# A sample's cache pages in a hybrid decoder step: all key scores ahead of most value pages, low parts through PSUM

## The chip, the cores and the metric

The kernel runs on 1 core of one Trainium2 chip. The metric is the device time of one execution in microseconds (us), the median of several. One profiled execution has its own time, and the tables say which of the two a number is.

## The reference

One step of a two-layer decoder: a Mamba-2 layer and an FFN, then one shared key/value projection, differential attention over it, and a second FFN. It computes this for a prompt of 16 + 512 tokens and for 8 sample tokens. Each sample token also attends to its past of 2048 tokens, which lies in a paged cache, 16 pages of 128 tokens for keys and as many for values, so 128 key pages and 128 value pages in all.

```python
def swiglu(x, w_gate, w_up, w_down):
    return (jax.nn.silu(x @ w_gate) * (x @ w_up)) @ w_down

def diff_attn_sample(h, k_past, v_past, k_new, v_new, pos, w_q, lam_vecs, subln_w, w_o, lambda_init):
    q = rotary((h @ w_q).reshape(b, T, DIFF_HEADS, 2, DIFF_QK_DIM), pos)
    s_past = jnp.einsum('bqhcd,bkhcd->bhcqk', q, k_past) * scale
    s_new = jnp.einsum('bqhcd,bkhcd->bhcqk', q, k_new) * scale
    w = diff_weights(jnp.concatenate([s_past, s_new], axis=-1), lam)   # softmax, map 0 - lam * map 1
    o = (jnp.einsum('bhqk,bkhe->bqhe', w[..., :P], v_past)
         + jnp.einsum('bhqk,bkhe->bqhe', w[..., P:], v_new))
    return diff_output(o, subln_w, w_o, lambda_init)
...
    # layer 0: mamba2, post_norm, swiglu, post_norm -> shared_kv
    # layer 1: attention, post_norm, swiglu, post_norm
```

## The kernel before

Activations are stored transposed: 128 partitions by T = 536 columns (528 prompt, 8 sample). A matrix product of full precision is made of three passes over rounded operands, high by high, low by high and high by low (`unit`, L121). For that each weight tile of up to 128x1024 comes as `raw` by a DMA of ACT's queue (L192), ACT copies it to `whi` with rounding (L200), and DVE, or POOL during the attention, subtracts: `wlo` = `raw` - `whi` (L202). Activations are split alike by `split`, high part on ACT (L242), low part on DVE (L243).

An FFN stage is one block of 128 hidden columns: the gate's product in PSUM, Silu on ACT into `sg` (L919), the up product in PSUM, `sg` times that product on DVE back into `sg` (L925), and the split of `sg`. The down products are added to the residual on DVE (L871, L872, in the last group L941) and shifted (L255); sums for the norm go on DVE or POOL (L268, L269). The norm `ln` subtracts and scales (L288, L290), applies weight and bias (L303) and makes high and low parts (L305), the latter as `x2lo` for the attention.

The sample tokens run ahead of the prompt: `early` takes their columns through the first FFN and the query projection while the prompt is still behind, and then starts `decode`. That is a generator with one step for each page. A step loads key page n+2 into one of 3 slots (a DMA of SP), multiplies key page n by the broadcast query on POOL (L1152), sums over 64 elements on DVE into the score tile `sc` (L1153), and takes value page n-24 (3 slots of its own) with four matmuls into PSUM bank `ps_e` (L125; the trace shows 8 records for a page). Every 16 key pages a softmax over them is spawned (L1174 to L1191), every 16 value pages the output of a sample is copied out (L1204).

The order on PE, DVE, ACT and POOL is made at build time: generators carry a modelled PE time, and whatever is behind it is pumped (here 3.2 for each step of `decode`) between the groups of the main flow, then a scheduler with priorities arranges each engine's row. SP's row is in program order. On the chip each engine takes its row in order and waits on semaphores.

`attention` takes heads 0 to 7: projections of k, v, q, rotation (L1348 to L1351), the split of `qk`, the score maps, the values. At its start the phase "attn" moves low parts of weights to POOL. Before the product with `w_o` it must have all of `decode` behind it: the operands `ohi` and `olo` lie in the same memory as the page slots (`r5`, `dd`). The end of the sample's attention (`fin`, L1513 to L1545) is joined within the `w_o` stage.

Of the kernel before, what the change touches and what calls it, by code (L numbers as in the profile page):

```python
# [10 lines left out]
F32 = mybir.dt.float32  # L11
# [4 lines left out]
ALU = mybir.AluOpType  # L16
AX = mybir.AxisListType.X
# [3 lines left out]
P = 128  # L21
# [12 lines left out]

NE = 24
MSP = 15

ES0 = 24

# [71 lines left out]
class Kernel:  # L111
# [68 lines left out]
    def wensure(self, load, split):  # L180
        nc = self.nc
        while self.wload < min(load, len(self.wq)):
            name, m, k0, k1 = self.wq[self.wload]
            n = k1 - k0
            mw = 32 if name == "w_dt" else P
            raw = self.wpool.tile([P, 8, P], F32, tag="raw", name="raw", bufs=3)
            if n == 2:
                n = 8
                src = self.i[name][m:m + 4][:, :, k0:k1, :].rearrange("m p k c -> p m (k c)")
                nc.scalar.dma_start(out=raw.rearrange("p (m k) c -> p m (k c)", k=2), in_=src)  # L190
            else:
                nc.scalar.dma_start(out=raw[:, :n, :mw], in_=self.i[name][m][:, k0:k1, :])  # L192
            self.wt[self.wload] = (raw, n, mw)
            self.wload += 1
        while self.wsplit < min(split, len(self.wq)):
            raw, n, mw = self.wt[self.wsplit]
            hi = self.wpool.tile([P, 8, P], F32R, tag="whi", name="whi", bufs=4)
            lo = self.wpool.tile([P, 8, P], F32R, tag="wlo", name="wlo", bufs=4)
            r = raw[:, :n, :mw]
            nc.scalar.copy(hi[:, :n, :mw], r)  # L200
            eng = self.lo_engine()
            eng.tensor_tensor(out=lo[:, :n, :mw], in0=r, in1=hi[:, :n, :mw].bitcast(F32), op=ALU.subtract)  # L202
            self.wt[self.wsplit] = (hi, lo, n, mw)
            self.wsplit += 1

# [128 lines left out]
    def build(self):  # L334
        nc, tc = self.nc, self.tc
        with ExitStack() as ctx:
            self.cp = ctx.enter_context(tc.tile_pool(name="const", bufs=1))
            self.wpool = ctx.enter_context(tc.tile_pool(name="wts", bufs=1))
            self.rp = ctx.enter_context(tc.tile_pool(name="regions", bufs=1))
            self.dp = ctx.enter_context(tc.tile_pool(name="scratch", bufs=1, space=DRAM))  # L340
            self.pp = ctx.enter_context(tc.tile_pool(name="psum", bufs=1, space=PSUM))
            self.gi, self.gn = 0, 3
            self.wi = 0
            self.lnps = "ab"
            self.lastexp = None
            self.phase = "mixer"
            self.wplan()
            self.consts()
            with tc.tile_pool(name="mixer", bufs=1, side="right") as mp:
                self.mp = mp  # L350
                self.mixer()
            with tc.tile_pool(name="rest", bufs=1, side="right") as sp:
                self.sp = sp
                self.rest()
# [432 lines left out]
    def rest(self):  # L787
# [52 lines left out]
            t2[0] = self.region("R6", [P, 8, T], F32, "t1")  # L840
            return t2[0]

        gens = self.ffn(x1k, FW, mk_t0, lnf0, gens, after_first=lnps, lasth=FH)
        S.finish(self.early_gen)

        self.attention(x2, gens)
# [27 lines left out]
    def proj(self, groups, xk, halves, evac, lnf, lasth=None):  # L874


        gens = []
        for gi, grp in enumerate(groups):
            last = gi == len(groups) - 1
            chs = [self.wget(nc_) for _, nc_ in grp]  # L880
            if not last:
                self.wahead(min(2, 4 - sum(n for _, n in grp)))
            for hf, (c0, n) in enumerate((lasth or halves) if last else halves):
                for (m, _), ch in zip(grp, chs):
                    ps = self.gps()
                    self.unit(ps, ch, xk, (c0, n))
                    evac(m, ps, c0, n)
                if last:
                    gens.append(self.S.spawn(lnf(hf, c0, n)) if lnf else None)
        self.wahead(2)  # L890
        return gens

    def ffn(self, xk, halves, mk_t, lnf, gens, after_first=None, lasth=None, regs=("R0", "R1")):
        nc, S, sp = self.nc, self.S, self.sp
        V, A = nc.vector, nc.scalar
        t = None
        for part in range(2):
# [5 lines left out]
            j = 0  # L903
            while j < 11:
# [5 lines left out]
                for hf, (c0, n) in enumerate((lasth or halves) if first else halves):  # L910
                    if first:
                        S.finish(gens[hf])
                        if hf == 1 and after_first is not None:
                            after_first()
                    for jj, (cg, cu) in zip(grp, chs):
                        pg, pu = self.gps(), None
                        self.unit(pg, [cg], xk, (c0, n))
                        sg = self.scr(n)
                        si = A.activation(sg, pg[:, :n], AF.Silu)  # L919
                        if self.lastexp is not None:  # L920
                            self.order(self.lastexp, si)
                            self.lastexp = None
                        pu = self.gps()
                        self.unit(pu, [cu], xk, (c0, n))
                        V.tensor_tensor(out=sg, in0=sg, in1=pu[:, :n], op=ALU.mult)  # L925
                        hh, hl = hk(jj)
                        self.split(hh[:, c0:c0 + n], hl[:, c0:c0 + n], sg)
                if first:
                    self.wahead(2)
                j += len(grp)  # L930
# [13 lines left out]
            if part == 0:  # L944
                self.proj([[(m, 2)] for m in range(8)], hk, halves, evac, None)
            else:
                gens = self.proj([[(m, 2)] for m in range(6)] + [[(6, 2), (7, 2)]], hk, halves, evac, lnf, lasth)
        return gens


# [48 lines left out]
    def early(self, t):  # L999
# [103 lines left out]
        for j in range(4):  # L1103
            nc.sync.dma_start(out=bass.AP(tensor=q.tensor, offset=q.offset + 256 * j, ap=[[1024, 8], [1, 256]]),
                              in_=qr[32 * j:32 * j + 8, :])
        yield 3.0
        self.dec_gen = S.spawn(self.decode(), 0.0)

    def page(self, cache, n, slot):
# [3 lines left out]


    def decode(self):
        nc, S, i, sp = self.nc, self.S, self.i, self.sp
        V, A, G = nc.vector, nc.scalar, nc.gpsimd
        kslot = self.kslot
        vslot = [self.r5[:, 1, :], self.r5[:, 2, :], self.r5[:, 3, :]]
        qslot = [self.dd[:, 2, :], self.dd[:, 3, :]]  # L1120
        self.Mb = sp.tile([P, 8, 16], F32, name="Mb", tag="Mb")
        self.Sb = sp.tile([P, 8, 16], F32, name="Sb", tag="Sb")
        self.oT = sp.tile([P, 8, 16], F32, name="oT", tag="oT")
        kq, vq = {}, {}
        N = 128

        def qload(b):
            q = self.scr_q
# [4 lines left out]
        VL = 24  # L1133
        w = {}
        sc = None
        qload(0)
        for n in range(N + VL + 1):
            if n < N:
                b, p = divmod(n, 16)
                if p == 8 and b < 7:  # L1140
                    qload(b + 1)
                if p == 0:
                    sc = sp.tile([P, 288], F32, tag="sc", name="sc", bufs=3)
                    V.memset(sc[:, 256:], 0.0)
                if n + 2 < N:
                    page("cache_k", n + 2, kslot[(n + 2) % 3])
            v = n - VL
            if 0 <= v + 2 < N:
                page("cache_v", v + 2, vslot[(v + 2) % 3])
            if n < N:  # L1150
                kt = kslot[n % 3]
                G.tensor_tensor(out=kt, in0=kt, in1=qslot[b % 2], op=ALU.mult)  # L1152
                V.reduce_sum(sc[:, 16 * p:16 * p + 16], kt.rearrange("p (c d) -> p c d", d=64), axis=AX)  # L1153
            if v >= 0 and v < N:
                bv, pv = divmod(v, 16)
                if pv == 0:
                    pe = self.ps("e")
                vt = vslot[v % 3]
                for j in range(4):
                    self.mmf(pe[32 * j:32 * j + 32, :256], w[bv][:, 16 * pv:16 * pv + 32],  # L1160
                             vt[:, 256 * j:256 * j + 256], start=pv == 0, stop=pv == 15, share=4)
                if pv == 15:
                    S.spawn(self.dec_out(bv, pe), 0.5)
            yield 3.2
            if n < N and p == 15:
                w[b] = sc
                S.spawn(self.dec_softmax(b, sc), 0.0)

    def dec_softmax(self, b, sc):
        nc, sp = self.nc, self.sp  # L1170
# [36 lines left out]
    def attention(self, x2, gens):  # L1207
# [1 line left out]
        V, A, G = nc.vector, nc.scalar, nc.gpsimd  # L1209
        self.gn = 2  # L1210
        self.gi = 0
        self.phase = "attn"
        self.xi = 0
        a4 = self.four("R4a", F32, "att4")
        b4 = self.four("R4b", F32, "att4b")
# [57 lines left out]
        for h in range(8):  # L1273
            if h == 0:
                chs = [self.wget(1) for _ in range(3)]
                for hf in range(2):
# [3 lines left out]
                    V.tensor_tensor(out=x2["l"][:, :, d], in0=x, in1=x2["h"][:, :, d].bitcast(F32), op=ALU.subtract)  # L1280
                    for wi in range(3):
                        kvq(h, wi, chs[wi], hf)
            else:
                for wi in range(3):
                    ch = self.wget(1)
# [371 lines left out]
```

## Time and profile before

| | us |
|---|---|
| median of 3 executions | 1830.72 (1823.65 to 1832.97) |
| profiled execution | 1819.79 |
| its span | 1818.0 |
| PE busy in it | 1667.7 (92%) |
| DVE busy | 1169.8 (64%) |
| ACT busy | 768.3 (42%) |
| POOL busy | 572.6 (31%) |
| mean granted TensorE clock | 0.958 |

The page multiplications begin at 614 us and end near 1157; the first FFN's matmuls end near 994; the norm runs to 1051; head 0 takes until about 1120, the other heads to 1320, `w_o` and its norm to 1440, and the second FFN from there to 1800. Busy shares of PE overlap: a matmul is recorded for longer than the next one waits for it.

### The profile page before, as it was taken

The numbers are of one execution on the slowest core, as the hardware profiler recorded it, in microseconds if no ns is written. First come the engines' busy times: TensorE is split into PE (matmuls) and PEld (weight loads), VectorE is DVE, ScalarE is ACT, GpSimd is POOL, SyncE is SP. The second block draws the span as 40 slices with busy tenths as digits, with TensorE's granted clock in tenths as the row PEclk, the third lists the DMA queues.
The fourth block names the chain that finished last, engine by engine and source line by source line (L and its number), as shares of the span: only waits on it lengthen the run. The fifth ranks groups of instructions, "written<-read, shape, count | busy, mean of one in ns | idle before, by whom it ended". The sixth has DMA issues, their size and how long they took to land.

```text
span 1818.0 us, 32096 instructions
## 1 busy us (share of the span) xinstructions
PE 1667.7 (92%) x12232; PEld 1404.1 (77%) x12232; DVE 1169.8 (64%) x1837; ACT 768.3 (42%) x1578; POOL 572.6 (31%) x402
## 2 busy tenths in 40 slices
PE   7799998989999989999998686999987999999996
PEld 7788887877776766666666473679976899999995
DVE  5498877854362589966677969757778533443334
ACT  6978868252352322222223322455644432223223
POOL 0010011100150487555678485412225400000025
PEclk9899999999999999999999696999999999999998
DMA  5675565397969679989898586761202222332221
GB/s 179 164 220 184 174 205 178 131 218 271 314 205 378 213 247 360 346 306 332 315 326 312 193 329 220 277 225 68 72 31 81 71 93 72 92 117 93 76 81 55
DMA packets 156801, 355.50 MB, mean 196 GB/s; under 512 B 23509, under 2 KB 74118, under 8 KB 156518
## 3 DMA queue, kind: packets, MB, share of 16 engines
q1 hardware_dynamic: 116902, 228.26, 37.7%
q10 hardware_dynamic: 36944, 116.59, 19.1%
q0 software_dynamic: 2800, 8.60, 1.4%
q8 instruction: 96, 1.57, 0.3%
q14 instruction: 59, 0.48, 0.1%
HBM read 337.07 MB, written 16.52 MB: 194 GB/s over the span
## 4 chain that ended last, share of the span: by engine, by line
PE 60%; DVE 17%; DMA 8%; ACT 7%; POOL 4%; issue 4%; SPq 1%; ACTq 0%; POOLq 0%; DVEq 0%
PE ps_g L121 48%; PE ps_e L125 3%; DVE sc L1153 2%; PE ps_a L125 2%; DVE wlo L202 2%; PE ps_d L125 2%; ACT acsb L677 1%; PE ps_c L125 1%; DMA out_conv_s<-cv 1%; DMA acsb<-scr_chk 1%; POOL dd L1152 1%; POOL ln_xf L303 1%; ACT whi L200 1%; PE ps_b L121 1%; DMA dd<-in_cache_k 1%
## 5 line engine op out<-in xcount | busy, mean ns | idle before, releaser
L200 ACT CAST whi<-raw 128x1024 fp32r<-128x1024 f32 (+3 forms) x243 | 234.6, 967 | 476.1 <-PE ps_g L121 404.4
L202 DVE TENSOR_TENSOR wlo<-raw,whi 128x1024 fp32r<-128x1024 f32 (+2 forms) x211 | 276.7, 1313 | 200.1 <-ACT whi L200 197.2
L1152 POOL TENSOR_TENSOR dd<-dd 128x1024 f32<-128x1024 f32 x85 | 215.8, 2543 | 102.7 <-DMA dd<-in_cache_k 88.4
L121 PE MATMUL ps_g<-xhi,whi 128*128 128x268 f32 (+1 forms) x656 | 194.9, 297 | 14.3 <-ACT xhi L242 9.4
L121 PE MATMUL ps_g<-x3hi,whi 128*128 128x260 f32 x704 | 200.1, 285 | 3.8 <-ACT sgw L919 3.3
L121 PE MATMUL ps_g<-x3lo,whi 128*128 128x260 f32 x704 | 199.5, 284 | 0.3 <-POOL x3lo L305 0.3
L121 PE MATMUL ps_g<-x3hi,wlo 128*128 128x260 f32 x704 | 199.1, 283 | 0.0
L121 PE MATMUL ps_g<-xhi,wlo 128*128 128x268 f32 (+1 forms) x656 | 196.5, 300 | 0.0
L121 PE MATMUL ps_g<-xlo,whi 128*128 128x268 f32 (+1 forms) x656 | 194.0, 296 | 0.1
L121 PE MATMUL ps_g<-x1hi,whi 128*128 128x512 f32 (+1 forms) x384 | 148.2, 386 | 4.1 <-ACT sgw L919 4.1
L121 PE MATMUL ps_g<-x1lo,whi 128*128 128x512 f32 (+1 forms) x384 | 148.6, 387 | 3.3 <-POOL x1lo L305 3.2
L121 PE MATMUL ps_g<-x1hi,wlo 128*128 128x512 f32 (+1 forms) x384 | 147.3, 384 | 0.0
L1152 POOL TENSOR_TENSOR r<-r,dd 128x1024 f32<-128x1024 f32 x43 | 107.8, 2508 | 113.9 <-DMA dd<-in_cache_k 75.7
L121 PEld LDWEIGHTS ps_g<-xhi,whi 128*128 128x128 f32 (+1 forms) x656 | 125.6, 192 | 22.7 <-ACT xhi L242 9.4
L121 PEld LDWEIGHTS ps_g<-x3hi,whi 128*128 128x128 f32 x704 | 132.8, 189 | 4.5 <-ACT sgw L919 3.7
L121 PEld LDWEIGHTS ps_g<-x3lo,whi 128*128 128x128 f32 x704 | 133.3, 189 | 0.5 <-POOL x3lo L305 0.5
L121 PEld LDWEIGHTS ps_g<-x3hi,wlo 128*128 128x128 f32 x704 | 133.5, 190 | 0.0
L121 PEld LDWEIGHTS ps_g<-xhi,wlo 128*128 128x128 f32 (+1 forms) x656 | 125.2, 191 | 7.5 <-issue 7.1
L121 PEld LDWEIGHTS ps_g<-xlo,whi 128*128 128x128 f32 (+1 forms) x656 | 125.6, 191 | 3.9 <-issue 2.8
L121 PE MATMUL ps_g<-hlo,whi 128*128 128x260 f32 (+2 forms) x400 | 126.7, 317 | 0.0
L121 PE MATMUL ps_g<-hhi,whi 128*128 128x260 f32 (+2 forms) x400 | 126.2, 316 | 0.0
L121 PE MATMUL ps_g<-hhi,wlo 128*128 128x260 f32 (+2 forms) x400 | 126.2, 316 | 0.0
(523 smaller groups left out, 4181.0 us busy)
## 6 DMA issues: line engine op xcount, KB each, us to landing
r<-in_cache_v SPq DMA_DIRECT2D x128, 512.0 KB, 5.1
dd<-in_cache_k SPq DMA_DIRECT2D x85, 512.0 KB, 5.3
raw<-in_w_gate ACTq DMA_DIRECT2D x44, 512.0 KB, 3.8
raw<-in_w_up ACTq DMA_DIRECT2D x44, 512.0 KB, 5.7
r<-in_cache_k SPq DMA_DIRECT2D x43, 512.0 KB, 5.3
raw<-in_w_in ACTq DMA_DIRECT2D x40, 512.0 KB, 3.8
raw<-in_w_down ACTq DMA_DIRECT2D x32, 384.0 KB, 3.3
raw<-in_w_down ACTq DMA_DIRECT2D x32, 320.0 KB, 5.4
```

The costliest lines, as they stand in the source:

```text
L121: return self.nc.tensor.matmul(out, lhsT=l, rhs=r, start=start, stop=stop)
L125: return self.nc.tensor.matmul(out, lhsT=l, rhs=r, start=start, stop=stop)
L200: nc.scalar.copy(hi[:, :n, :mw], r)
L202: eng.tensor_tensor(out=lo[:, :n, :mw], in0=r, in1=hi[:, :n, :mw].bitcast(F32), op=ALU.subtract)
L303: E1.tensor_scalar(out=xf, in0=t3[:, k, :], scalar1=w, scalar2=b, op0=ALU.mult, op1=ALU.add)
L677: A.activation(L[:n, h, :], L[:n, h, :], AF.Relu, scale=-1.0, bias=self.acs[:n, c, 8 * g + h:8 * g + h + 1])
L1152: G.tensor_tensor(out=kt, in0=kt, in1=qslot[b % 2], op=ALU.mult)
L1153: V.reduce_sum(sc[:, 16 * p:16 * p + 16], kt.rearrange("p (c d) -> p c d", d=64), axis=AX)
```

## The change

`decode` is rewritten. Key pages come one for each step of 2.7, and from page 24 on every 4th step takes one value page, with two value slots. After the last key page the slots of keys and queries join the free list, seven in all, and the value pages that are left are taken two for each step of 4.6, loaded up to six ahead. Since all eight samples' scores now live at once, `room` finds memory for them: three `sc` tiles, columns of the former third value slot, and a tile `sch`.

In both FFNs DVE writes the product of gate and up back to PSUM, and `split` reads it there. From the start of `decode` to the last down group of the first FFN (`wps`), ACT also copies each raw weight tile in pieces of at most 512 columns to PSUM banks `ps_a` and `ps_b`, and DVE subtracts from there. From that last group's first half to the end of head 0's projections (`hold`) `decode` stands still before its next key page; then `hold` ends and the phase "attn" begins, later than before.

```diff
@@ wensure
-            eng = self.lo_engine()
-            eng.tensor_tensor(out=lo[:, :n, :mw], in0=r, in1=hi[:, :n, :mw].bitcast(F32), op=ALU.subtract)
+            if self.wps:
+                for x in range(0, n, 4):
+                    y = min(x + 4, n)
+                    pw = self.ps("ab"[x // 4])[:, :P * (y - x)].rearrange("p (k c) -> p k c", c=P)
+                    nc.scalar.copy(pw, r[:, x:y, :])
+                    nc.vector.tensor_tensor(out=lo[:, x:y, :], in0=pw, in1=hi[:, x:y, :].bitcast(F32), op=ALU.subtract)
+            else:
+                eng = self.lo_engine()
+                eng.tensor_tensor(out=lo[:, :n, :mw], in0=r, in1=hi[:, :n, :mw].bitcast(F32), op=ALU.subtract)
@@ proj, after evac
+                if last and hold:
+                    self.hold, self.wps = True, False
@@ ffn
-                        V.tensor_tensor(out=sg, in0=sg, in1=pu[:, :n], op=ALU.mult)
+                        V.tensor_tensor(out=pu[:, :n], in0=sg, in1=pu[:, :n], op=ALU.mult)
                         hh, hl = hk(jj)
-                        self.split(hh[:, c0:c0 + n], hl[:, c0:c0 + n], sg)
+                        self.split(hh[:, c0:c0 + n], hl[:, c0:c0 + n], pu[:, :n])
@@ early, end
+        self.wps = True
         self.dec_gen = S.spawn(self.decode(), 0.0)
@@ decode
-        vslot = [self.r5[:, 1, :], self.r5[:, 2, :], self.r5[:, 3, :]]
+        vfree = [self.r5[:, 1, :], self.r5[:, 2, :]]
+        def room(b):
+            if b < 3:
+                sc = sp.tile([P, 288], F32, tag="sc", name="sc", bufs=3)
+            elif b < 6:
+                sc = self.r5[:, 3, 288 * (b - 3):288 * (b - 2)]
+            else:
+                if b == 6:
+                    st["h"] = sp.tile([P, 2, 288], F32, name="sch", tag="hE")
+                sc = st["h"][:, b - 6, :]
+            V.memset(sc[:, 256:], 0.0)
+            return sc
+        def vload(upto):
+            while st["load"] < min(upto, N) and vfree:
+                vs[st["load"]] = vfree.pop(0)
+                page("cache_v", st["load"], vs[st["load"]])
+                st["load"] += 1
+        def value():
...
+            for j in range(4):
+                self.mmf(pe[32 * j:32 * j + 32, :256], w[bv][:, 16 * pv:16 * pv + 32],
+                         vt[:, 256 * j:256 * j + 256], start=pv == 0, stop=pv == 15, share=4)
+            vfree.append(vt)
+            if pv == 15:
+                S.spawn(self.dec_out(bv, pe), 0.5)
         qload(0)
-        for n in range(N + VL + 1):
...
-            yield 3.2
+        for n in range(N):
+            while self.hold:
+                yield 0.5
...
+            if n >= VL0 and (n - VL0) % VL1 == 0:
+                vload(st["use"] + 2)
+                value()
+            elif n == VL0 - VL1:
+                vload(1)
+            kt = kslot[n % 3]
+            G.tensor_tensor(out=kt, in0=kt, in1=qslot[b % 2], op=ALU.mult)
+            V.reduce_sum(sc[:, 16 * p:16 * p + 16], kt.rearrange("p (c d) -> p c d", d=64), axis=AX)
+            yield 2.7
...
+        vfree += kslot + qslot
+        while st["use"] < N:
+            for _ in range(2):
+                if st["use"] < N:
+                    vload(st["use"] + 6)
+                    value()
+            yield 4.6
@@ attention
-        self.phase = "attn"
...
                     for wi in range(3):
                         kvq(h, wi, chs[wi], hf)
+                self.hold = False
+                self.phase = "attn"
```

DVE's row in the second half of the first FFN, where down products alternate with weights' low parts and key reductions. Before:

```order
L871 SCALAR_TENSOR_TENSOR t_6913<-x1hi,ps_g_7056 128x512
L202 TENSOR_TENSOR wlo<-raw,whi 128x640
L872 SCALAR_TENSOR_TENSOR t_6913<-x1lo,t_6913 128x512
L255 TENSOR_TENSOR t_6913<-t_6913,stk 128x512
L1153 TENSOR_REDUCE sc<-r_5412 128x16
L202 TENSOR_TENSOR wlo<-raw,whi 128x768
L1153 TENSOR_REDUCE sc<-dd 128x16
```

And now, where `t_7033` is the same residual tile:

```order
L881 SCALAR_TENSOR_TENSOR t_7033<-x1hi,ps_g_7183 128x512
L1200 TENSOR_REDUCE sc<-r_5412 128x16
L208 TENSOR_TENSOR wlo<-ps_a,whi 128x512
L882 SCALAR_TENSOR_TENSOR t_7033<-x1lo,t_7033 128x512
L208 TENSOR_TENSOR wlo<-ps_b,whi 128x256
L1200 TENSOR_REDUCE sc<-dd 128x16
L264 TENSOR_TENSOR t_7033<-t_7033,stk 128x512
L208 TENSOR_TENSOR wlo<-ps_a,whi 128x512
L208 TENSOR_TENSOR wlo<-ps_b,whi 128x128
L1200 TENSOR_REDUCE sc<-dd 128x16
```

Each low part stands now in two pieces that read `ps_a` and `ps_b`, and three key reductions stand where two did.

DVE's row at the end of the norm, where head 0's keys and queries (`att`) are rotated; `rot` is scratch. Before:

```order
L1348 STREAM_SHUFFLE rot<-att_10908 128x268
L1153 TENSOR_REDUCE sc<-r_5412 128x16
L1153 TENSOR_REDUCE sc<-dd 128x16 x2
L1153 TENSOR_REDUCE sc<-r_5412 128x16
L1153 TENSOR_REDUCE sc<-dd 128x16 x2
L1349 TENSOR_TENSOR att_10908<-att_10908,att_10903 128x268 x2
L1350 TENSOR_TENSOR rot<-rot,att_10903 128x268 x2
```

And now:

```order
L314 TENSOR_TENSOR x2lo<-ln_xf,x2hi 128x256 x4
L1393 STREAM_SHUFFLE rot<-att_10404 128x268
L1394 TENSOR_TENSOR att_10404<-att_10404,att_10399 128x268
L1395 TENSOR_TENSOR rot<-rot,att_10399 128x268
L1396 TENSOR_TENSOR att_10404<-att_10404,rot 128x268
```

The key reductions no longer stand between the first shuffle and the rotation; ten of them come later, within heads 0 and 1.

PE's row just ahead of the first `w_o` matmuls (operands `ohi`, `olo`). Before:

```order
L121 MATMUL ps_g_14571<-x2hi,whi 128x264
L121 MATMUL ps_g_14571<-x2lo,whi 128x264
L121 MATMUL ps_g_14571<-x2hi,wlo 128x264
L121 MATMUL ps_g_14626<-ohi,whi 128x260
L121 MATMUL ps_g_14626<-olo,whi 128x260
```

And now:

```order
L131 MATMUL ps_g_14988<-c_ident,att_10404 128x128 x2
L131 MATMUL ps_g_14988<-c_ident,att_10404 16x128
L127 MATMUL ps_e<-r_5412,sch 32x256 x8
L127 MATMUL ps_e<-dd,sch 32x256 x4
L123 MATMUL ps_b<-qk_10403 128x512
L123 MATMUL ps_g_15192<-ohi,whi 128x260
```

The last value pages (`ps_e`, four matmuls a page) stand directly ahead of `w_o` now, and of the 128 pages 102 stand behind what ran after 1120 us before.

## Rows read from the trace of the kernel before

**Rows 1.** Windows: us, busy us (records) by engine, granted clock, DMA share, GB/s.

```profile
614.00:690.00 76.00, 69.85 (x301) 55.26 (x300) 65.50 (x53) 20.58 (x26) 66.42 (x26) 0.98 0.76 247
690.00:956.00 266.00, 264.96 (x1433) 180.03 (x1432) 201.32 (x191) 69.60 (x88) 165.87 (x69) 1.00 0.92 331
956.00:994.00 38.00, 37.95 (x278) 29.12 (x276) 28.68 (x29) 11.42 (x19) 30.61 (x17) 1.00 0.89 330
994.00:1054.00 60.00, 34.61 (x214) 22.73 (x215) 57.86 (x74) 19.89 (x39) 33.06 (x15) 0.69 0.64 212
1054.00:1120.00 66.00, 44.83 (x346) 33.35 (x346) 48.26 (x82) 15.10 (x37) 50.78 (x27) 0.76 0.80 283
1120.00:1220.00 100.00, 94.55 (x811) 69.22 (x809) 70.46 (x149) 42.27 (x145) 36.34 (x22) 0.97 0.77 261
1220.00:1320.00 100.00, 99.14 (x836) 92.75 (x834) 72.49 (x200) 61.59 (x217) 24.85 (x20) 1.00 0.19 67
```

Its columns of engines are PE, PEld, DVE, ACT, POOL.

**Rows 2.** The same windows, instructions on tile ps_e alone (PE, PEld, DVE, ACT).

```profile
690.00:956.00 266.00, 38.98 (x488) 9.60 (x488) 0.00 (x0) 1.12 (x3) 1.00 0.92 331
956.00:994.00 38.00, 6.39 (x80) 1.57 (x80) 0.00 (x0) 0.37 (x1) 1.00 0.89 330
994.00:1054.00 60.00, 9.05 (x80) 1.85 (x80) 0.00 (x0) 0.35 (x1) 0.69 0.64 212
1054.00:1120.00 66.00, 9.88 (x96) 2.11 (x96) 0.00 (x0) 0.00 (x0) 0.76 0.80 283
1120.00:1220.00 100.00, 22.95 (x272) 5.61 (x272) 0.00 (x0) 1.10 (x3) 0.97 0.77 261
```

**Rows 3.** Timeline of PE in the FFN: start, us, instruction.

```profile
803.67 0.39 PE L121 MATMUL ps_g<-x1hi,whi 128*128 128x512 f32 x1
804.00 0.64 PE L125 MATMUL ps_e<-r,sc 128*32 128x256 f32 x8
804.56 0.50 PE L121 MATMUL ps_g<-x1lo,whi 128*128 128x512 f32 x1
```

**Rows 4.** Windows of 40 us, columns as in the first group.

```profile
620.00:660.00 40.00, 40.00 (x175) 32.48 (x174) 35.01 (x26) 9.66 (x12) 34.15 (x13) 1.00 0.76 248
780.00:820.00 40.00, 40.00 (x217) 27.24 (x216) 27.94 (x27) 12.03 (x14) 22.45 (x9) 1.00 0.90 312
```

**Rows 5.** Groups by line, 620 to 960: count, busy, mean ns, idle before, releasers.

```profile
L1152 POOL TENSOR_TENSOR dd<-dd 128x1024 f32<-128x1024 f32 x58 | 148.8, 2567 | 85.8 <-DMA dd<-in_cache_k 74.3 <-DVE sc L1153 6.0 <-DVE wlo L202 2.0
L202 DVE TENSOR_TENSOR wlo<-raw,whi 128x1024 fp32r<-128x1024 f32 (+2 forms) x57 | 92.3, 1619 | 18.6 <-ACT whi L200 16.6 <-DMA raw<-in_w_gate 1.3
L1153 DVE TENSOR_REDUCE sc<-dd 128x16 f32<-128x1024 f32 x58 | 70.1, 1210 | 13.4 <-POOL dd L1152 13.4
```

**Rows 6.** Timeline of DVE in the FFN, where POOL is idle from 805.42 to 808.03.

```profile
805.40 0.69 DVE L925 TENSOR_TENSOR sgw<-sgw,ps_g 128x512 f32<-128x512 f32 x1 [0.83 <-PE ps_g L121]
806.34 1.22 DVE L202 TENSOR_TENSOR wlo<-raw,whi 128x1024 fp32r<-128x1024 f32 x1
807.47 0.68 DVE L243 TENSOR_TENSOR hlo<-sgw,hhi 128x512 fp32r<-128x512 f32 x1
```

**Rows 7.** Timeline of DVE from the norm to head 0's rotation.

```profile
1002.15 8.94 DVE L290 TENSOR_TENSOR t<-t,ln_rs 128x512 f32<-128x512 f32 x4
1012.48 2.48 DVE L288 TENSOR_TENSOR t<-t,ln_md 128x512 f32<-128x512 f32 x4
1049.14 1.96 DVE L305 TENSOR_TENSOR x2lo<-ln_xf,x2hi 128x256 fp32r<-128x256 f32 x2
1060.16 1.22 DVE L1153 TENSOR_REDUCE sc<-dd 128x16 f32<-128x1024 f32 x1 [5.50 <-POOL dd L1152]
1078.29 1.82 DVE L1349 TENSOR_TENSOR att<-att,att 128x268 f32<-128x268 f32 x2
```

**Rows 8.** DMA issues, 620 to 690: count, KB each, median us to landing.

```profile
dd<-in_cache_k SPq DMA_DIRECT2D x16, 512.0 KB, 4.2
```

**Rows 9.** The same of 850 to 940.

```profile
dd<-in_cache_k SPq DMA_DIRECT2D x15, 512.0 KB, 7.2
```

More of the change, by code (lines that the diff above doesn't have):

```diff
@@ L36 @@
 MSP = 15
+VL0, VL1 = 24, 4
 ES0 = 24
@@ L342, in build @@
             self.gi, self.gn = 0, 3
+            self.hold = self.wps = False
             self.wi = 0
@@ L841, in mk_t0 @@
             return t2[0]
-        gens = self.ffn(x1k, FW, mk_t0, lnf0, gens, after_first=lnps, lasth=FH)
+        gens = self.ffn(x1k, FW, mk_t0, lnf0, gens, after_first=lnps, lasth=FH, hold=True)
         S.finish(self.early_gen)
@@ L872, in resid, with proj @@
         V.scalar_tensor_tensor(out=tv, in0=xl.bitcast(F32), scalar=ALPHA, in1=tv, op0=ALU.mult, op1=ALU.add)
-    def proj(self, groups, xk, halves, evac, lnf, lasth=None):
+    def proj(self, groups, xk, halves, evac, lnf, lasth=None, hold=False):
         gens = []
@@ L891, in proj, with ffn @@
         return gens
-    def ffn(self, xk, halves, mk_t, lnf, gens, after_first=None, lasth=None, regs=("R0", "R1")):
+    def ffn(self, xk, halves, mk_t, lnf, gens, after_first=None, lasth=None, regs=("R0", "R1"), hold=False):
         nc, S, sp = self.nc, self.S, self.sp
@@ L946, in ffn @@
             else:
-                gens = self.proj([[(m, 2)] for m in range(6)] + [[(6, 2), (7, 2)]], hk, halves, evac, lnf, lasth)
+                gens = self.proj([[(m, 2)] for m in range(6)] + [[(6, 2), (7, 2)]], hk, halves, evac, lnf, lasth, hold)
         return gens
@@ L1123, in decode @@
         self.oT = sp.tile([P, 8, 16], F32, name="oT", tag="oT")
-        kq, vq = {}, {}
         N = 128
+        w, vs, st = {}, {}, {"load": 0, "use": 0, "pe": None}
+        def room(b):
[9 more added lines that the diff above has]
+            return sc
         def qload(b):
@@ L1132, in decode @@
         page = self.page
-        VL = 24
-        w = {}
-        sc = None
-        qload(0)
-        for n in range(N + VL + 1):
[L1138 to L1163, printed above, removed]
-            yield 3.2
-            if n < N and p == 15:
@@ new lines, in vload @@
+        def vload(upto):
[4 more added lines that the diff above has]
+        def value():
+            v = st["use"]
+            st["use"] += 1
+            bv, pv = divmod(v, 16)
+            if pv == 0:
+                st["pe"] = self.ps("e")
+            pe, vt = st["pe"], vs.pop(v)
+            for j in range(4):
[4 more added lines that the diff above has]
+                S.spawn(self.dec_out(bv, pe), 0.5)
@@ new lines, in decode @@
+        qload(0)
+        for n in range(N):
+            while self.hold:
+                yield 0.5
+            b, p = divmod(n, 16)
+            if p == 8 and b < 7:
+                qload(b + 1)
+            if p == 0:
+                sc = room(b)
+            if n + 2 < N:
+                page("cache_k", n + 2, kslot[(n + 2) % 3])
+            if n >= VL0 and (n - VL0) % VL1 == 0:
[7 more added lines that the diff above has]
+            yield 2.7
+            if p == 15:
```

## The prediction

> **What bounds the kernel now.** I read first the busy columns by stage [rows 1], then the value pages in the same stages [rows 2], and then single stretches. From 690 to 994 PE is nearly never idle: 264.96 of 266 us in the FFN's long part, with 61 value pages in it (488 records, 8 a page). In the norm and before head 0 PE is busy 34.61 of 60 and 44.83 of 66 at granted clocks of 0.69 and 0.76, and DVE is busy 57.86 of 60: there DVE's row sets the pace. From 1120 on the heads fill PE again. So a page's matmuls cost time in the FFN and with the heads, and key work costs it in the norm and before head 0.
>
> **Durations.** Through the FFN a 512-column matmul takes 40/175 = 0.23 us [rows 4]. One with a value page behind it takes 804.56 − 803.67 = 0.89 [rows 3], so a page costs PE 0.66. A key page comes each 40/13 = 3.08 us in the first part and each 40/9 = 4.44 later [rows 4].
>
> **FFN, 614 to 956.** The order has 21 value pages in it where there were 62, and about 104 key pages where there were 88 (58 in two of the three slots from 620 to 960 [rows 5]). PE alone would need (301 + 1433 − 8 − 488) = 1238 matmuls [rows 1, 2] × 0.232 = 287 us, and 21 × 0.66 = 14, so 301 against 342 before: a gain of 41 at most. But DVE's row holds four key reductions in a gate and up stage now, and DVE takes its row in order: the gate-up product and the low parts stand behind reductions that wait for POOL, POOL waits for the key's DMA (74.3 us of its idle time) [rows 5]. So 104 keys times their period p is a second floor. At 3.08 it is 320 us, at 4.44 it would be 462. Which of them? A slot of three goes through landing, multiplication and reduction. Landing was 4.2 us in the early part [rows 8] and 7.2 late [rows 9], at 248 to 331 GB/s [rows 1, 4]. With 41 pages of 0.524 MB less and 16 more, 107 MB become 94, in some 325 us 290 GB/s, in the lower half between; I take 5.0 for landing. Multiplication is 2.4 to 2.6 [rows 5], reduction 1.21, and between and around them some 0.8 stay, an estimate from the early part: 3 × 3.08 − 4.2 − 2.57 − 1.21 = 1.26 is what was left there, with POOL contended. (5.0 + 2.45 + 1.21 + 0.8)/3 = 3.15. I take 3.15 × 104 = 328, a gain of **14**; bounds are the gain of 41 (PE's floor) and a loss of 32 (p = 3.6, which 1.4 us more of landing or of waiting in DVE's row would make).
>
> **Low parts in PSUM.** 57 low parts took 1.62 us in the mean [rows 5], while a 1024-column one takes 1.22 and a 512-column difference 0.68 with POOL idle beside them [rows 6]. So POOL's multiplications stretch DVE's differences of two SBUF operands, while the reductions, with one operand, stay at 1.21 [rows 5]. Two pieces of 0.68 make 1.36, if PSUM keeps them apart from POOL. DVE is then 57 × 0.26 = 15 us less busy, off its critical waits; POOL's mean falls from 2.57 toward 2.40. ACT gets two more copies for each tile of about 0.6 (an estimate from the gate-up difference's size), 57 × 1.2 = 68 us, hidden: ACT is busy 69.6 of 266 [rows 1]. I cost that at nothing beside p, where it is contained; if ACT's copies come late, the low part is late and PE waits for it, which is inside the loss named for p. The gate-up product took 0.69 with an operand in PSUM, and its split 0.68 without [rows 6], so for the second FFN, where POOL is idle for most of the time, I put zero.
>
> [...]
>
> **956 to 994.** 2 pages for 10 [rows 2] where PE is full: 8 × 0.66 = **5** gained, between 0 and 5.
>
> **Norm, 994 to 1054.** POOL's 15 instructions there [rows 1] are mostly key multiplications; in the changed order six key reductions are left ahead of the pause, about half, and POOL's low parts go. The four scalings L290 took 8.94 beside POOL, while four instructions of the same shape took 2.48 alone [rows 7]; that pair alone is 6.5. Half of the reductions, six again, is 7.3, and DVE is busy 57.86 of 60 [rows 1], so these come off its row. With other stretched steps and softmax pieces gone I take **20** off; bounds 8 (the reductions alone) and 25 (DVE's row without any key work).
>
> **Before head 0, 1054 to 1120.** After the last `x2lo` (1049.14 + 1.96 = 1051.1) rotation waits for seven key reductions and begins with L1349 at 1078.29; DVE idles first at 1060.16 − 5.50 = 1054.7 [rows 7]. PE has head 0's projections in that hole. Now the row goes straight on. What is late next is the projection itself: DVE cannot rotate before PE has it. PE's busy 44.83 contains 96 records of pages [rows 2] and projections at a clock of 0.76. Ten keys are still to run, behind rotation. I take **20**, between 10 and 25 (the hole, 1078.3 − 1054.7, and a little).
>
> **Moved value pages.** 102 pages stand behind 1120 where 34 stood (272 records [rows 2]). 68 × 0.66 = 45 us of PE if nothing takes them up. Counting every matmul's columns at 0.232 us per 512, the 200 us from 1120 to 1320 hold about 175 of PE work, so 25 are free, mostly in short pieces; I let a third of the 45 fall into them and into waits in head 0, and charge **28**, between 10 and 45. DMA does not stand against it: 0.19 busy from 1220 on [rows 1].
>
> **The end of the heads.** The last pages stand directly ahead of `w_o`, and the splits of `oF` cannot begin before the page slots, the same memory, are done: six splits of 0.68 [rows 6] are now in one row, 4 us, while before only the last stood there. The heads' matmuls that were mixed into `w_o` cover a part. I charge **4**, between −10 and 15.
>
> **Sum.** −14 − 5 − 20 − 20 + 28 + 4 = −27 against the profiled 1819.79: 1793. The median of the executions is 10.9 above the profiled one, so 1804 for the median, with about 1790 to 1820 for this case by itself.
>
> **Rivals.** *Keys set the pace of the FFN (slower).* If p is 3.6, that stage takes 374 instead of 342: −27 + 14 + 32 = +19, 1850. The mechanism is DVE's in-order row: four reductions a stage that wait for keys hold back the products for PE. For it: POOL's idle time is nearly all DMA [rows 5], and the later period was 4.44. Against: that period was seen with a value page beside each key and PE saturated, the early one is 3.08. It decides from p = 3.41, where the sum is zero. *Moved pages cost in full (no change).* 45 + 15 = 60 against gains of 59: 1831. For it: PE busy 94.55 and 99.14 of 100 [rows 1]. *PE is the FFN's only bound (a large gain).* p at 2.9 brings 41 instead of 14, so −54: 1777. For it: the 3.08 was itself measured with PE 40.00 of 40 busy. *PSUM doesn't part DVE and POOL, the change doesn't do what it says.* Then p stays near 3.3, the FFN gives nothing and the norm some 15: 0 − 5 − 15 − 20 + 32 = −8, 1823.
>
> **How the numbers follow.** 0.42 for the forecast, 0.13 for keys setting the pace, 0.15 for full cost of the moved pages, 0.20 for PE alone, 0.10 for no parting. 0.5% of the median is about 9 us, what a measurement of this kernel can tell from no change. Faster: 0.40 of the forecast, 0.20, 0.04 of no parting and 0.04 of the full cost = 0.68. Same: 0.02 + 0.05 + 0.09 + 0.04 of the slow rival = 0.20. Slower: 0.09 + 0.01 + 0.02 = 0.12. The range leaves out most of the slow rival (0.12) and the lower part of the large gain (0.08): 1774 to 1836.
>
> **What would show it.** In the changed profile: the first FFN's matmuls ending near 975 instead of 994 (14 and 5 us earlier), with a key period near 3.15 and POOL's multiplications near 2.45; low parts in two pieces of about 0.68 with no stretch; the norm in some 40 us, no key reduction between the first shuffle of head 0 and its rotation; value pages all through the heads, PE full to their end, and the first `w_o` matmuls near 1293 instead of 1320. A key period over 3.4, or heads longer by over 45 us, would make it wrong.

## The result

The changed kernel is slower: 1881.53 us median of 4 (1871.35 to 1886.11) against 1830.03 (1823.65 to 1832.97), a ratio of 1.0288 with a 95% interval of [1.0255, 1.032]. The profiled execution took 1885.24 us, its span is 1883.1 and its mean granted clock 0.953. Below, a run's median is given with the ratio to the kernel before, measured on the same chip in the same stretch of time.

The span, taken apart at the same points of both traces (us):

| stretch | before | after | difference |
|---|---|---|---|
| start to the first key multiplication | 614.0 | 622.1 | +8.1 |
| to the last down matmul on `hhi` of the first FFN | 377.3 | 358.9 | −18.4 |
| to the last `x2lo` of the norm | 59.8 | 51.1 | −8.7 |
| to head 0's first rotation product | 27.2 | 0.4 | −26.8 |
| to the first `w_o` matmul | 241.5 | 350.2 | +108.7 |
| to the end | 498.2 | 500.4 | +2.2 |

Three stretches, from the FFN to head 0's rotation, did what was forecast, or part of it: −53.9 us. The heads, from rotation to `w_o`, lost twice that. In the first row 3.9 of the 8.1 us are there before the first FFN's first matmul, and the start of the key loop lay between 615 and 625 us in all the runs below, so it is left out of the argument.

The windows of the changed kernel, columns as in [rows 1] (PE, PEld, DVE, ACT, POOL busy, clock, DMA share, GB/s):

```profile
690.00:946.00 256.00, 240.96 (x1112) 180.63 (x1111) 205.26 (x255) 115.83 (x181) 197.85 (x85) 0.98 0.83 292
982.00:1033.00 51.00, 21.71 (x107) 16.99 (x106) 48.32 (x80) 19.11 (x39) 19.50 (x9) 0.63 0.32 111
1033.00:1100.00 67.00, 53.74 (x406) 48.39 (x406) 56.88 (x81) 19.94 (x53) 41.50 (x23) 0.90 0.49 174
1100.00:1180.00 80.00, 75.84 (x672) 51.56 (x664) 43.55 (x114) 35.64 (x126) 14.53 (x11) 0.94 0.86 311
1180.00:1380.00 200.00, 193.35 (x1477) 130.04 (x1479) 82.33 (x247) 74.85 (x255) 28.76 (x26) 0.99 0.53 198
```

and the instructions on `ps_e` alone in the last three (PE, PEld, DVE, ACT), as in [rows 2]:

```profile
1033.00:1100.00 67.00, 2.61 (x30) 0.68 (x32) 0.00 (x0) 0.00 (x0) 0.90 0.49 174
1100.00:1180.00 80.00, 23.18 (x288) 5.80 (x280) 0.00 (x0) 0.74 (x2) 0.94 0.86 311
1180.00:1380.00 200.00, 65.36 (x500) 16.02 (x504) 0.00 (x0) 1.49 (x4) 0.99 0.53 198
```

In the FFN PE is no longer full (240.96 of 256, against 264.96 of 266 in [rows 1]); from 1180 on it is. But a page there takes 65.36 × 8/500 = 1.05 us of recorded PE time, where it took 38.98 × 8/488 = 0.64 in the FFN of before [rows 2]. PE's timeline shows why:

```profile
1190.06 0.28 PE L123 MATMUL ps_g<-x2hi,whi 128*128 128x264 f32 x1
1190.27 0.62 PE L127 MATMUL ps_e<-r 128*32 128x256 f32 x2
1190.82 0.39 PE L123 MATMUL ps_g<-x2lo,whi 128*128 128x264 f32 x1
1191.13 0.62 PE L127 MATMUL ps_e<-r 128*32 128x256 f32 x2
1191.68 0.39 PE L123 MATMUL ps_g<-x2hi,wlo 128*128 128x264 f32 x1
1192.00 0.62 PE L127 MATMUL ps_e<-r 128*32 128x256 f32 x2
```

The four matmuls of a page use 32 columns of the array each (128*32) and run side by side when they stand together: 8 records in 0.64 us in [rows 3]. Here each stands alone between two of a head's projections. A lone one (2 records) lasts as long as the four together, and from the projection ahead of it to the one behind it go 0.76 to 0.87 us where 0.12 are one projection's own. In the heads' row 55 of the pages' matmuls stand alone. (The counts of 62, 21 and 7 in the expectations hold 7 short matmuls on the same bank more, which the traces show ahead of the key loop and which are no pages.)

SP's timeline of the same place (start, us, what it issues) shows a second thing:

```profile
1186.55 0.35 SPq L1125 DMA_DIRECT2D dd<-in_cache_v  x1
1200.31 0.35 SPq L1414 DMA_DIRECT2D out_k<-att  x1
1216.03 0.35 SPq L1415 DMA_DIRECT2D out_v<-vf  x1
1217.23 1.53 SPq L1125 DMA_DIRECT2D dd<-in_cache_v  x2
```

No page is loaded from 1186.9 to 1217.2: SP's row is in program order, and a head's writes of k and v stand in it behind its rotation, ahead of the next pages. The chain of waits has such a piece in each of the last four heads:

```profile
1218.40 6.95 DMA dd<-in_cache_v
1270.17 7.34 DMA dd<-in_cache_v
1320.41 6.76 DMA dd<-in_cache_v
1373.28 8.35 DMA dd<-in_cache_v
```

### The profile page after: what moved, and what is told of

Its sections match the earlier page's. It is cut to its first block, busy times and chain, and to the rows that moved or that the text cites. A ratio compares the mean times of both kernels' runs of the same rounds, so it can differ in the third digit from the quotient of the medians.

```text
span 1883.1 us, 32307 instructions
## 1 busy us (share of the span) xinstructions
PE 1707.3 (91%) x12232; PEld 1427.8 (76%) x12232; DVE 1128.5 (60%) x1904; ACT 835.1 (44%) x1712; POOL 553.1 (29%) x401
## 4 chain that ended last, share of the span: by engine, by line
PE 50%; DVE 16%; DMA 15%; ACT 7%; POOL 7%; issue 4%; SPq 1%; ACTq 0%; POOLq 0%; DVEq 0%
PE ps_g L123 38%; PE ps_e L127 4%; DMA dd<-in_cache_k 4%; POOL dd L1199 3%; PE ps_a L127 2%; DMA dd<-in_cache_v 2%; POOL r L1199 1%; ACT acsb L687 1%; PE ps_d L127 1%; DMA out_conv_s<-cv 1%; PE ps_b L123 1%; DVE wlo L208 1%; DVE sch L1200 1%; DMA st<-in_state_ssm 1%; DVE wlo L211 1%
## 5 line engine op out<-in xcount | busy, mean ns | idle before, releaser
L211 DVE TENSOR_TENSOR wlo<-raw,whi 128x1024 fp32r<-128x1024 f32 (+3 forms) x146 | 173.7, 1191 | 161.0 <-ACT whi L202 160.6
L1199 POOL TENSOR_TENSOR dd<-dd 128x1024 f32<-128x1024 f32 x85 | 207.0, 2446 | 62.2 <-DMA dd<-in_cache_k 55.6
L211 POOL TENSOR_TENSOR wlo<-raw,whi 128x1024 fp32r<-128x1024 f32 (+1 forms) x31 | 70.3, 2270 | 291.0 <-ACT whi L202 231.4
```

## The experiments

Theories from the two traces: lone page matmuls cost 29 us in the heads; loads behind the writes cost some of the rest; the pause itself is worth its 36 us, or it isn't. The rival to all of these is the plain price of the pages that run from 1180 on, 62 × 0.66 us.

**no_pause.**

```diff
-        gens = self.ffn(x1k, FW, mk_t0, lnf0, gens, after_first=lnps, lasth=FH, hold=True)
+        gens = self.ffn(x1k, FW, mk_t0, lnf0, gens, after_first=lnps, lasth=FH)
```

> The changed kernel without the pause of the keys in the norm; its PE row has 21 lone page matmuls where the changed one has 62. If the pause is worth what the two traces show (norm 9 us shorter, the hole before head 0's rotation 27 us shorter) and the lone matmuls cost 29 us: 1881 + 36 - 20 = about 1897. If the hole only moved into the heads, so that the pause is worth nothing: 1881 - 20 = about 1861.

Measured: 1829.69 us, ratio 1.0 [0.9974, 1.0026]. Neither value: taking the pause out gives back 52 us, the whole loss. (Only 14 of the 55 lone matmuls are left in it, so two causes go at once.) The norm grows again (last `x2lo` 72 us behind the FFN, 51 with the pause), and so head 0's rotation is 17 us later (1049.9), but from there to `w_o` it takes 279.5 us instead of 350.2.

**pages_first.** The four matmuls get a scheduling priority by which they stay together; in its trace none of a page's stands alone.

```diff
             for j in range(4):
-                self.mmf(pe[32 * j:32 * j + 32, :256], w[bv][:, 16 * pv:16 * pv + 32],
-                         vt[:, 256 * j:256 * j + 256], start=pv == 0, stop=pv == 15, share=4)
+                with self.tc.high_priority(offset=3000):
+                    self.mmf(pe[32 * j:32 * j + 32, :256], w[bv][:, 16 * pv:16 * pv + 32],
+                             vt[:, 256 * j:256 * j + 256], start=pv == 0, stop=pv == 15, share=4)
```

> The changed kernel with a higher scheduling priority for the four matmuls of a value page: in PE's row 7 lone page matmuls are left of 62, and nothing waits that did not wait before. Lone matmuls cost 55 x 0.70 - 14 x 0.66 = 29 us: about 1852. If they only take PE time that would be idle anyway, since page loads come late behind the writes of k and v: 1875 to 1885.

Measured: 1853.88, ratio 1.0125 [1.0088, 1.0162]: 27.6 us off, by the price read from the trace (29). The changed kernel's first fault is settled: the row's order, not the number of pages. Up to the rotation nothing moved (1032.7 against 1032.5); rotation to `w_o` went from 350.2 to 317.0.

**quads** tried the same with a critical section around the four.

```diff
+            with self.tc.tile_critical():
-            for j in range(4):
+              for j in range(4):
```

> The changed kernel with the four matmuls of each value page kept adjacent on PE; nothing else differs. Split pages (62 lone page matmuls in PE's row, about 55 of them within the heads, cost 0.70 us each in the trace, as much as a whole page of four that run side by side): the heads get shorter by 55 x 0.70 - 14 x 0.66 = 29 us, 1881 falls to about 1852, and no page costs more than 0.9 us with the step around it. Late loads (page loads stand behind the writes of k and v on SP): the heads still wait for the pages, 1875 to 1885. Plain price of the moved pages (62 x 0.66): unchanged too, 1875 to 1885.

Measured: 2354.24, ratio 1.2877 [1.2839, 1.2915]. It tells nothing of lone matmuls: the section made every page wait for other engines. PE's waits in it (waiting for what: us, times, longest):

```profile
PE ps_e L127 <- issue: 159.5, 47, 16.4
PE ps_e L127 <- DMA dd<-in_cache_v: 54.4, 14, 4.7
PE ps_e L127 <- DMA dd<-in_cache_k: 34.4, 3, 16.8
```

A page waits even for a key's load there, with which it has nothing to do.

**no_pause_pages_first** has both edits, no pause and the priority.

> The changed kernel without the pause and with the page matmuls kept together. 21 lone matmuls become 7: 14 x 0.70 - 3.5 x 0.66 = 7.5 us below the 1829.7 without the pause alone, about 1822. If the lone ones cost nothing, 1826 to 1833.

Measured: 1825.44, ratio 0.9971 [0.9951, 0.999]; the step from `no_pause` is 4 us, less than 7.5 and within the intervals of both. So with the pages together the pause costs 1853.9 − 1825.4 = 28 us.

**pages_first_writes_on_pool.**

```diff
-        nc.sync.dma_start(out=self.o["k"][h], in_=kf)
-        nc.sync.dma_start(out=self.o["v"][h], in_=vf)
+        nc.gpsimd.dma_start(out=self.o["k"][h], in_=kf)
+        nc.gpsimd.dma_start(out=self.o["v"][h], in_=vf)
```

> As pages_first, and the heads' writes of k and v are issued by POOL's queue instead of SP's, so that page loads do not stand behind them. If late loads hold the heads (four stretches of 7 us of value DMA on the chain of the changed kernel, 16 us between a k write and the next load): 20 to 30 us below pages_first. If PE's own work holds the heads: within 8 us of pages_first.

Measured: 1836.09, ratio 1.0039 [1.0014, 1.0065]: 18 us below `pages_first`. But it moved more than the writes: with SP's row free, the scheduler put 7 of the 10 keys behind the pause back into the norm (last `x2lo` at 1057.0 instead of 1032.3), so it undid most of the pause as well. The next two keep the writes on SP.

**pages_first_writes_later** and **no_pause_writes_later** issue the two writes on SP, after a head's first block of scores.

```diff
         for b in range(5):
             if b == 1:
+                nc.sync.dma_start(out=self.o["k"][h], in_=kf)
+                nc.sync.dma_start(out=self.o["v"][h], in_=vf)
                 while self.hvals < h:
```

> As pages_first, with the pause, and each head's writes of k and v issued by SP after the head's first block of scores instead of right behind its rotation, so that SP's queue does not stand still for them ahead of the loads of pages. 7 of the 10 key pages stay behind the pause (in the run with the writes on POOL 7 of the 10 went back into the norm). If the pause costs 28 us because key and value loads queue behind those writes: 1830 to 1838, with the last key before 1080 us. If the pause costs because ten keys and the values start later at all: 1848 to 1856.

> As no_pause_pages_first, with the writes of k and v issued later as in pages_first_writes_later. If late value loads cost the heads time without the pause too (5.6% of the heads' chain is value DMA, 18 us): 1810 to 1820. If PE is full in the heads without the pause: 1822 to 1828.

Measured: 1845.82, ratio 1.0119 [1.0083, 1.0156], and 1817.89, ratio 0.9952 [0.9931, 0.9972]. Between these two the pause still costs 28 us. By the medians each is about 8 us below its partner with the early writes, but the partners ran in another stretch of time; by the ratios it is 1 and 3.5 us, and the intervals overlap. Nor did the edit free SP's row, as it was meant to: in `pages_first_writes_later` the next load still stands behind both writes.

```profile
1235.41 0.35 SPq L1513 DMA_DIRECT2D out_k<-att  x1
1243.98 0.35 SPq L1514 DMA_DIRECT2D out_v<-att4b  x1
1245.17 0.35 SPq L1125 DMA_DIRECT2D r<-in_cache_v  x1
```

From 1030 to 1350 SP waited 111 us at the writes, where it waited 114 in `pages_first` (101 and 124 without the pause). Three of the ten keys also went back into the norm (1012.6 to 1022.2), and the last key came at 1088 us, not before 1080. From rotation to `w_o` it took 307.0 us for 317.0 with the pause, but 265.3 for 266.7 without. What the writes ahead of loads cost is therefore not shown by these runs. The first time lies between the two that were expected, which left the pause's price open; the second lies where late loads were to put it, but not by the heads.

**pages_first_no_products** leaves out the matmuls of 89 of the 102 pages taken after the last key, and keeps their loads; the sample's attention lacks these pages.

```diff
-            for j in range(4):
+            for j in range(4 if n < N - 1 or pv in (0, 15) else 0):
```

> As pages_first, but of the pages taken after the last key only the first and the last of each sample are multiplied: 89 pages' matmuls are left out, their loads stay. If PE is full in the heads, 89 x 0.66 = 59 us come off: about 1795. If a third of the pages falls into idle PE time, as the prediction had it: 39 us, about 1815. If the heads wait for page loads rather than for PE, under 20 us: 1835 or more.

Measured: 1800.12, ratio 0.9856 [0.9823, 0.9889], 53.8 us below `pages_first`: 0.60 us for each page left out, nine tenths of 0.66. By the ratios it is 49 us, 0.55 a page. So PE time that was idle or waiting in the heads takes up a tenth to a sixth of the moved pages, not a third.

**values_each_key** puts the pages back beside the keys, with the pause in place.

```diff
-VL0, VL1 = 24, 4
+VL0, VL1 = 24, 1
```

> The changed kernel with one value page behind every key page from page 24 on (VL1 = 1 instead of 4), so that 104 value pages run beside keys and 24 are left; 7 lone page matmuls. If pages cost PE 0.66 wherever PE is full and the excess in the heads is lone matmuls and late loads: the FFN gets some 40 us longer, the heads some 80 to 90 shorter, 1830 to 1845. If value loads beside keys slow the keys (3 us to 4.3 a page), the FFN gets 80 to 100 us longer and the time is 1880 or more.

Measured: 1853.23, ratio 1.0131 [1.0099, 1.0162], between the two expectations. The FFN got 8 us longer, not 40 (last down matmul at 988.9); keys went back to 4.4 us a page, so that 93 were begun by then. The 35 that were left ran until 1142, beside lumps of 8 pages in PE's row, and head 0's first rotation product came only at 1166.0. PE's waits from 985 to 1200:

```profile
PE ps_e L127 <- DMA r<-in_cache_v: 44.5, 25, 6.8
```

**pause_with_values** and **pause_with_values_dense** are `pages_first_writes_later` with only the keys paused (2.0 and 1.0 between pages).

```diff
             while self.hold:
-                yield 0.5
+                if st["use"] < 16 * (len(w) - 1):
+                    vload(st["use"] + 2)
+                    value()
+                    yield 2.0
+                else:
+                    yield 0.5
...
-            if n >= VL0 and (n - VL0) % VL1 == 0:
+            if n >= VL0 and ((n - VL0) % VL1 == 0 or self.phase == "attn"):
```

> As pages_first_writes_later, but only the keys pause: value pages of the samples whose scores are done are taken during the pause (one each 2.0 of modelled PE time) and one beside each of the ten keys behind it; 21 pages stand in PE's row from the norm to head 0 where 3 stood. If the pause costs 28 us because no value page may run until the last key, while PE is idle for some 60 us between 980 and 1100: 1846 - 28 = about 1818, and below it by what the shorter norm keeps (up to 15), so 1803 to 1820. If it costs because ten keys are multiplied beside the heads: 1838 to 1848.

> The same with one value page each 1.0 of modelled PE time during the pause; of the pages 14 more stand in head 1's part, and none in the last three heads. If pages only have to come early to fill idle PE time: at or below pause_with_values, 1795 to 1820. If the denser row makes PE wait for loads with its heads' products behind (one lump of 14 pages): 1820 to 1835.

Measured: 1820.75, ratio 0.9948 [0.9927, 0.9969], and 1868.82, ratio 1.0214 [1.0182, 1.0246]. With values in the pause 25 of its 28 us come back (31 by the ratios), though the ten keys are still beside the heads. PE in the two stretches (columns as above), `pages_first_writes_later` first,

```profile
982.00:1100.00 118.00, 73.74 (x495) 62.82 (x499) 108.83 (x166) 37.66 (x91) 59.87 (x30) 0.74 0.46 161
```

and `pause_with_values`:

```profile
982.00:1100.00 118.00, 80.99 (x627) 60.41 (x625) 96.56 (x160) 43.19 (x105) 55.60 (x29) 0.82 0.65 225
```

PE has 132 more records there, and DMA moves 225 GB/s for 161. That settles what the pause cost: it stopped the values with the keys, since one generator takes both and all but 26 pages stand behind the last key, and PE, DMA and the page slots were partly idle in it. How the 25 us divide was not tested. The records are some 16 pages, about 11 us of PE at 0.66; the rest can be loads that came earlier, for SP's waits at the writes fell with it, from 111 to 36 us (1030 to 1350).

The dense version shows the other end: two slots can't feed a page each 1.0, and a lump of 14 pages in PE's in-order row holds the heads' products behind it (39.7 us of waits for `r<-in_cache_v` from 1000 to 1380). SP's row holds up more than pages: the load of the cosine table stands behind 18 value loads, and head 0's rotation on DVE waits 25.26 us for it.

```profile
1008.73 51.56 SPq L1125 DMA_DIRECT2D r<-in_cache_v  x18
1060.39 0.58 SPq L1268 DMA_DIRECT2D att<-in_cos  x1
1065.62 0.78 DVE L1400 TENSOR_TENSOR att<-att,att 128x268 f32<-128x268 f32 x2 [25.26 <-DMA att<-in_cos]
```

**no_psum**, **before_psum** and **before_psum_writes_later** test the PSUM operands. The first takes them out of the changed kernel,

```diff
-        self.wps = True
...
-                        V.tensor_tensor(out=pu[:, :n], in0=sg, in1=pu[:, :n], op=ALU.mult)
+                        V.tensor_tensor(out=sg, in0=sg, in1=pu[:, :n], op=ALU.mult)
...
-                        self.split(hh[:, c0:c0 + n], hl[:, c0:c0 + n], pu[:, :n])
+                        self.split(hh[:, c0:c0 + n], hl[:, c0:c0 + n], sg)
```

the second puts only these edits into the kernel before, and the third adds the later writes to that.

> The changed kernel with low parts of weights and of the gate-up product read from SBUF as before. If PSUM operands free DVE and POOL from each other, the key period of the first FFN goes from 3.1 to about 3.5 us and the FFN ends 15 to 35 us later, 1896 to 1916 in all; if they are worth nothing, the time stays at 1875 to 1888. The heads stay as they are by either.

> The kernel before with only the PSUM edits: low parts of weights (from the start of decode to the last down group of the first FFN) and of the gate-up product read from PSUM. The first FFN was full on PE in the kernel before (264.96 of 266 us), so freer DVE and POOL can only help ahead of it and in its few stalls: 1815 to 1828. If the two more copies on ACT or the banks ps_a and ps_b make weights late: over 1835.

> As before_psum, with the writes of k and v issued later. The key loop of the kernel before runs to 1157 us, beside heads 0 to 2, and its loads stand behind the same writes: if that holds heads 0 to 2, 1808 to 1817; if not, 1818 to 1824.

Measured: `no_psum` 1892.78, ratio 1.0341 [1.03, 1.0383], 11 us above the changed kernel; `before_psum` 1821.14, ratio 0.9953 [0.9934, 0.9972]; with the later writes 1817.01, ratio 0.9941 [0.9922, 0.9961], a step of 4 us by the medians and 2 by the ratios, not clear of noise. PSUM operands are worth 8 to 11 us. What they do is plain in the groups by line from 620 to 960 (busy, mean ns, idle before). The changed kernel:

```profile
L1199 POOL TENSOR_TENSOR dd<-dd 128x1024 f32<-128x1024 f32 x71 | 171.7, 2432 | 47.3 <-DMA dd<-in_cache_k 40.8 <-DVE t L881 4.1 <-DVE r L1200 1.3
L208 DVE TENSOR_TENSOR wlo<-ps_a,whi 128x512 fp32r<-128x512 f32 x60 | 40.8, 680 | 2.6 <-ACT whi L202 2.5
L207 ACT COPY ps_a<-raw 128x512 f32<-128x512 f32 x60 | 35.4, 591 | 90.3 <-DVE wlo L208 90.2
L252 DVE TENSOR_TENSOR hlo<-ps_g,hhi 128x512 fp32r<-128x512 f32 x11 | 7.5, 677 | 0.0
```

and `no_psum`:

```profile
L1198 POOL TENSOR_TENSOR dd<-dd 128x1024 f32<-128x1024 f32 x68 | 178.8, 2638 | 58.8 <-DMA dd<-in_cache_k 46.3 <-DVE r L1199 4.1 <-DVE wlo L211 2.4
L211 DVE TENSOR_TENSOR wlo<-raw,whi 128x1024 fp32r<-128x1024 f32 (+2 forms) x54 | 92.0, 1704 | 0.1
L252 DVE TENSOR_TENSOR hlo<-sgw,hhi 128x512 fp32r<-128x512 f32 x11 | 21.1, 1922 | 0.0
```

With an operand in PSUM a 512-column difference takes 0.68 us in the mean, as long as one alone in [rows 6], while POOL multiplies keys beside it (busy 266.50 of these 340 us); without it `hlo` of the same size takes 1.92, and a whole low part of up to 1024 columns 1.70. ACT's copies, 0.59 us each for 512 columns, are hidden: ACT is busy 151.99 of the 340 us. In the FFN more hangs on the operands than the 11 us: without them a key takes (931.3 − 615.0)/93 = 3.40 us instead of the changed kernel's 3.12, and the last `hhi` matmul comes at 1008.2 instead of 981.0. Of these 27 us the stretch to head 0's rotation gives 9 back and the rest of the profiled execution 4.

**no_pause_third** and **pause_with_values_third** put 7 pages back into the FFN's idle PE time.

```diff
-VL0, VL1 = 24, 4
+VL0, VL1 = 24, 3
```

> As no_pause_writes_later, with one value page for every third key page in the first FFN instead of every fourth (31 pages there instead of 24). PE stands idle for some 30 us of the first FFN in the changed kernel, since keys set its pace: if these take the 7 pages, 4 to 8 us come off, 1810 to 1815; if value loads slow the keys, the time stays or rises, 1818 to 1826.

> As pause_with_values, with one value page for every third key page in the first FFN. By the same reasoning 1812 to 1818 if idle PE time in the FFN takes the pages, 1820 to 1828 if value loads slow the keys.

Measured: 1813.86, ratio 0.9921 [0.9898, 0.9945], and 1809.78, ratio 0.9906 [0.9882, 0.993]. Set against their partners by ratio (0.9952 and 0.9948, from other stretches of chip time) they gain some 6 and 8 us, with intervals that overlap; it points to idle PE time in the FFN taking the pages. `pause_with_values_third` is 17 us under the kernel before, the fastest of those that compute everything.

## Why the prediction was wrong

The forecast was 1804 with a range to 1836; 1881 lies outside, on the other side.

- **FFN and 956 to 994: right.** −18.4 us against −14 − 5. From key 1 to key 94 the loop took (912.7 − 622.1)/93 = 3.12 us a page, against the 3.15 that was taken; keys, not PE, set the pace, and the slow rival (3.6) did not come; with SBUF operands the period was 3.40. The FFN ended at 982 and not near 975, because 8 us were lost ahead of the key loop. The floor of PE was put some 4 us too high (0.232 a matmul, where 40/175 is 0.2286), on which nothing hangs.
- **Low parts in PSUM: right.** POOL's multiplications took 2.43 us in the mean instead of 2.57, and a piece of 512 columns with its operand in PSUM 680 ns in the mean, as long as the difference of two SBUF operands that took 0.68 us with POOL idle in [rows 6].
- **Norm: half.** −8.7 for −20, near the lower bound of 8. The scaling that was 8.94 beside POOL in [rows 7] went, but another took its place, 7.83 us at 983.91 for four subtractions that took 2.48 alone:

```profile
983.91 7.83 DVE L297 TENSOR_TENSOR t<-t,ln_md 128x512 f32<-128x512 f32 x4
```

  POOL worked beside it on the norm's sums, a key and a weight's low part (982.86 to 991.2), and five key multiplications that stand ahead of the pause ran on POOL after 985.
- **Hole before head 0: right in place, wrong in worth.** −26.8 for −20, a little beyond the bound of 25. But what ran in the hole before (projections and 12 pages, [rows 2]) was no waste, and the prediction charged nothing for taking it out.
- **Moved pages: the step that failed.** 28 us, between 10 and 45. Three things were left out of it. Price: 0.66 us holds for four adjacent matmuls, and the order as built, which was there to be read, has 55 lone ones in the heads; 28 us. Time: pages can be taken only where their loads and the generator let them, and the pause shut them out between 982 and 1100, where PE has idle time; 28 us, of which 25 came back when values went on in it. Queue: "DMA does not stand against it" was read from the share (0.19) [rows 1], not from SP's row, where writes that wait for a rotation hold the loads: from 1030 to 1350 SP waited 138 us at them, 99 in the kernel before. What this adds by itself stays open, since no run took the writes away from the loads and left the keys where they were. The filling by a third was a tenth to a sixth, so some 7 to 10 us of the 45 went uncharged.
- **End of the heads.** `w_o` to the end changed by 2.2 us; the charge of 4 is not contradicted.

By the runs' medians the loss adds up as steps: 1829 before; 1821 with the PSUM operands; 1825 with keys first and most values behind them, kept together and without the pause; 1854 with the pause; 1882 with lone matmuls. The slower rival that was priced, keys setting the pace of the FFN, is not what happened; a rival that the order of a page's own matmuls would have shown was not among them. Why the scheduler splits some pages and not others was not settled; the lone matmuls stand between 1180 and 1320, behind the gaps in the loads.

## What to carry to other kernels

Price a moved piece of work by the row in which it will stand, not by the row from which it comes: whether its instructions stay adjacent, which in-order queue issues its loads and what waits there. A pause meant for one engine's work should stop only that work; here DVE's norm wanted the keys away, and the values, on whose tile `ps_e` neither DVE nor POOL has a record from 690 us to 1220 in the kernel before (DVE x0 in [rows 2]), were stopped with them. An idle stretch that a change removes may have been covering something, so ask what ran in it and where that goes.

## What was not expected of the hardware

A lone 128*32 matmul of 256 columns in fp32 cost PE 0.64 to 0.75 us between two projections, as much as four of them that stand together (8 records in 0.64 us, [rows 3]): a page split into four has four such prices, and PE does not show as idle for it (193.35 of 200 us busy from 1180 on). And beside POOL's key multiplications `hlo` took DVE 0.677 us with one operand in PSUM, against 1.92 with both in SBUF, a greater stretch than the 1.62 over 1.22 from which it was forecast.
